# State space layer of a decoder trunk: response matrices stored lag by lag, their loads a tile ahead, prep's small products in fours

## The chip, the cores and the metric

The kernel runs on one core of a Trainium2 chip. The metric is the time of one execution on the device in microseconds (us). Three runs of the kernel before took 2993.37, 2993.86 and 2994.96 us; the median is 2993.86 us.

## The reference

The network is a trunk of two layers over 256 tokens of width 2048. Each layer has a token mixer, a cross-attention to a memory of 256 rows and a squared-ReLU MLP of width 8192. Layer 0's mixer is a gated MLP over chunks; layer 1's is a state space layer, and the change is there alone. Cut to that mixer:

```python
def s5_glu(h, w_in, lam_re, lam_im, log_dt, bm_re, bm_im, cm_re, cm_im, d_skip, w_out, b_out):
    u = (h @ w_in).reshape(bsz, seq, 128, 16)              # 128 groups of 16 channels
    lam = lax.complex(jnp.minimum(lam_re, -1e-4), lam_im)  # 128 x 64 states
    lam_bar = jnp.exp(lam * jnp.exp(log_dt)[:, None])
    b_bar = ((lam_bar - 1.0) / lam)[..., None] * bmat
    bu = jnp.einsum('gpc,bsgc->sbgp', b_bar, u)
    states[s] = lam_bar * states[s - 1] + bu[s]            # a scan over the tokens
    y = jnp.einsum('gcp,sbgp->bsgc', cmat, states).real + d_skip * u
    val, gate = jnp.split(gelu(y) @ w_out + b_out, 2, axis=-1)
    return val * jax.nn.sigmoid(gate)
```

## The kernel before

**The weight stream.** Every large product streams its weights in tiles of 256 rows by 512 columns (512 KB). For each tile, SP loads `wraw` (four buffers), ACT writes the rounded high part `whi` (L97), DVE the remainder `wlo` (L98; three buffers each), and PE multiplies in three passes. A tile costs 24 matmuls of 256 columns in `gemm_feat` (L159) and 12 matmuls of 512 columns in `gemm_tok` (L140 to L142) and `gemm_hid` (L552 to L554). After each tile, `tick` traces what is due beside the stream: pieces that `at(delay, fn)` planned for that count of tiles, and one queued piece of `self.side`, with a priority lowered by `lag`.

**What sets the order.** A scheduler places the instructions of each engine by these priorities and its own estimate of readiness. The order within an engine is then fixed; waits on semaphores are added where one engine needs another.

**Preparation.** `ssm_prep` queues the state space's matrices beside layer 0's MLP. A scan over chunks of T = 8 tokens needs three kinds of matrices, made for 32 quads (one group of 16 channels from each of four channel tiles) and kept in DRAM, two quads to a DRAM tile: `Pd` (inputs of a chunk to its state), `Qd` (state to outputs) and `Kd` (the response inside a chunk, 15 lags of 16 x 16, seven of them zero). In `quad_q`, DVE makes `qt` in three steps (L781 to L783), PE multiplies it with `bb` in four small products (L792), one into each strip of 32 rows of a PSUM tile; ACT and DVE copy them to `kd` (L796, L797), and POOL stores `kd` (L799): 128 rows of 240 numbers, a run of 960 bytes each. Only 16 rows of each 32 are read later. The same POOL queue zeroes the next `kd` (L795), loads the inputs `bcq` (L762) and stores `Qd` and `Pd` (L789, L810).

**The layer.** In `s5`, four chunks of 512 columns of `b_w_in` are streamed, eight weight tiles each, and the chain of chunk n runs beside the stream of the next one: `inputs`, `own` (products with `pq`, L874), `states`, `carry`, `outputs` (products with `dq`, L925, and with `qq`, L931), `features`. `own` and `outputs` load the matrices themselves where they are traced, through POOL (L832): `pq` from `Pd` (four buffers), `dq` from `Kd` (three) and `qq` from `Qd` (two), 512 KB each. `dq` is a Toeplitz matrix read out of `Kd` by an overlapping access pattern; each of its 128 rows is put together from eight runs of 512 bytes.

Of the kernel before, what the change touches and what calls it, by code (L numbers as in the profile page):

```python
# [9 lines left out]
F32 = mybir.dt.float32  # L10
# [6 lines left out]
P = 128  # L17
# [3 lines left out]
NB = 512  # L21
NCH = D // NB
KB = 2
# [6 lines left out]
T = 8  # L30
# [6 lines left out]
class Trunk:  # L37
    """Products run as three float32r passes over operands split exactly into a
    12-bit high part and the remainder; the residual stream stays on chip,
    token-major, and weights are streamed in chunks of KB x 128 rows by 512  # L40
    columns."""
# [26 lines left out]
    def later(self, n):  # L68
        """What is traced inside gives way to what the stream traces next."""
        return self.tc.high_priority(offset=-n)  # L70

    def at(self, delay, fn):
        """Trace fn after that many more pieces of the weight stream."""
        self.plan.append((self.now + delay, len(self.plan), fn))
        self.plan.sort(key=lambda p: p[:2])

    def tick(self):
        """Trace what is due beside the weight stream: planned pieces, then one queued piece."""
        self.now += 1
# [44 lines left out]
    def gemm_tok(self, act, w, n, acc=None, k0=0, kts=range(KT), first=True, last=True, raw=None):  # L124
        """acc[tok, t, col] (+)= act^T @ w[:, chunk n]"""
        nc = self.nc
        ah, al = act
        if acc is None:
            acc = self.psA.tile([P, 2, NB], F32, name="acc")
        out = acc if isinstance(acc, list) else [acc[:, t, :] for t in range(2)]  # L130
        kts = list(kts)
        for i in range(0, len(kts), KB):
            hi, lo = self.wtile(w, n, (k0 + kts[i]) // KB, raw)
            for kk in range(KB):
                kt = kts[i + kk]
                st = first and i == 0 and kk == 0
                en = last and i + kk == len(kts) - 1
                for t in range(2):
                    sl = slice(t * P, (t + 1) * P)
                    nc.tensor.matmul(out[t], ah[:, kt, sl], hi[:, kk, :], start=st, stop=False)  # L140
                    nc.tensor.matmul(out[t], ah[:, kt, sl], lo[:, kk, :], start=False, stop=False)  # L141
                    nc.tensor.matmul(out[t], al[:, kt, sl], hi[:, kk, :], start=False, stop=en)  # L142
            self.tick()
        return acc

    def gemm_feat(self, act, w, n):
        """acc[f, ft, tok] = (w[:, chunk n])^T @ act"""
        nc = self.nc
        ah, al = act
        acc = self.psA.tile([P, 4, S], F32, name="acc")  # L150
        for kc in range(KT // KB):
            hi, lo = self.wtile(w, n, kc)
            for kk in range(KB):
                kt = kc * KB + kk
# [46 lines left out]
    def transpose_chunk(self, src, gi, act, j, permute=False, halves=(0, 1)):  # L201
        """act[:, 4j..4j+3, :] = (src[tok, t, 512])^T * g, split"""
# [20 lines left out]
    def scale_chunk(self, src, gi, act, j):  # L223
        """act[:, 4j..4j+3, :] = src[feature, kt, token] * g, split"""
# [17 lines left out]
    def mem_stats(self, pool):  # L242
        """1/rms of each memory row, per partition and along the free axis"""
# [14 lines left out]
    def mem_prep(self, pool, layer):  # L258
        """Queue memory * g, feature-major, beside the stream; 1/rms comes later."""
# [320 lines left out]
    def exp(self, pool, x, shape, name, tag=None):  # L580
        """exp(x): n ln2 taken off in two exact parts, a polynomial, 2^n from the bits."""
# [22 lines left out]
    def cos_sin(self, pool, th, shape):  # L604
        """cos and sin: a multiple of pi/2 taken off in three parts, polynomials,
        then the quadrant's turn."""
# [37 lines left out]
    def ssm_prep(self, pool):  # L644
        """Queue the making of the chunked form of the state space, per group of 16 channels:
        Pd: lam^jr B_bar, rows (jr, c), from inputs of a chunk to its state;
        Qd: C lam^(j+1), columns (j, c), from the state before a chunk to its outputs;
        Kd: C lam^lag B_bar (+ d at lag 0), the response inside a chunk, after T-1 zero lags.
        A quad is one group of each 128-channel tile; two quads share a DRAM tile."""
# [7 lines left out]
        self.Kd = mk("Kd", [32, 2, 4, NL, 16])  # L657
# [81 lines left out]
        def last():  # L739
            """lam^8, lam^16, lam^32: over one, two and four chunks"""  # L740
# [14 lines left out]
        def cols(q):  # L755
            """the four groups of quad q: one in each 128-channel tile"""
            g0 = 32 * (q // 8) + q % 8
            return slice(g0, g0 + 25, 8)
# [26 lines left out]
        def quad_q(q):  # L785
# [5 lines left out]
            for g in range(4):  # L791
                nc.tensor.matmul(kp[32 * g:32 * g + 32], bb[:, g], qt[:, 0:T, g, :], start=True, stop=True,  # L792
                                 skip_group_check=True)
# [5 lines left out]
            nc.gpsimd.dma_start(out=self.Kd[q // 2][:, q % 2].rearrange("k t l c -> t k (l c)"), in_=kd)  # L799
# [22 lines left out]
    def s5(self, x, cur, nxt):  # L822
# [3 lines left out]
        with tc.tile_pool(name="s5", bufs=2, reuse_waits="tile") as sp:  # L826
# [3 lines left out]
            def load(src, nm):  # L830
                t = sp.tile([P, 2, 4, P], F32, name=nm, bufs={"pq": 4, "dq": 3, "qq": 2}[nm])
                nc.gpsimd.dma_start(out=t, in_=src)  # L832
                return t

            def chunks(n, acc):
                """Tokens to chunks: rows of u are (channel tile, chunk)."""
# [26 lines left out]
            def own(n):  # L863
                """each chunk's own part of its state"""
# [3 lines left out]
                for h in range(2):  # L868
                    pz = self.ps([P, 2, 2, 2, 64])
                    for i in range(2):  # L870
                        pq = load(self.Pd[4 * n + 2 * h + i], "pq")
# [8 lines left out]
            def states(n):  # L880
                """rows of vv are (odd group, state), real and imaginary apart"""
# [14 lines left out]
            def carry(n, c, k, by=1):  # L896
                """vv[c] += lam^(8 by) vv[c - by] for c, c + 2 by, ..., k of them"""
# [13 lines left out]
            def outputs(n, half):  # L911
# [4 lines left out]
                row = (2 * T - 1) * 16  # L916
                for i in (2 * half, 2 * half + 1):
                    kd = self.Kd[4 * n + i]
                    dq = load(bass.AP(tensor=kd.tensor, offset=kd.offset,
                                      ap=[[16, T], [8 * row, 16], [row, 8], [1, P]]), "dq")  # L920
                    qq = load(self.Qd[4 * n + i].rearrange("l p r n -> (l p) r n"), "qq")
                    qv = qq.rearrange("p r a b -> p r (a b)").rearrange("p r (j t c) -> p r t j c", t=4, c=16)
                    for l in range(2):
                        for t in range(4):
                            nc.tensor.matmul(py[l][32 * t:32 * t + 32, i, :], us[:, 2 * i + l, t, :], dq[:, l, t, :],  # L925
# [8 lines left out]
            def features(n):  # L934
                py = st.pop(n)[2]
                y = sp.tile([P, T, 4, 2, 16], F32, name="y", bufs=1)
# [11 lines left out]
            def follow(n):  # L948
                """the chain of channel tiles 4n..4n+3, laid beside the stream"""
# [10 lines left out]

            for n in range(NCH):
# [8 lines left out]
            for j in range(NCH):  # L970
# [20 lines left out]
                val = sp.tile([P, 2, NB], F32, name="val", bufs=1)  # L991
                gat = sp.tile([P, 2, NB], F32, name="gat", bufs=1)
# [14 lines left out]
class Norm:  # L1007
    """The RMSNorm of x that the next part reads: x is transposed and scaled by
    g chunk by chunk as it is finished; 1/rms comes later, per token."""
# [17 lines left out]
class FinalNorm:  # L1027
    """x * g and the sums of squares as the chunks of x are finished; then, per token tile,
    1/rms and the output."""
# [33 lines left out]
def regroup(tr, x):  # L1063
    """x in the order the state space wants: row (q, c) of tile h is token 8c + 4h + q."""
# [43 lines left out]
def chunked(w):  # L1108
    """[..., K, N] -> [..., N / 512, K / (KB 128), 128, KB, 512]"""
# [51 lines left out]
```

## Time and profile before

| | |
|---|---|
| median of three runs | 2993.86 us |
| span of the profiled execution, first to last instruction | 2994.1 us |
| time of PE, DVE, ACT, POOL busy | 2924.3, 1769.5, 1312.2, 168.9 us |
| mean granted TensorE clock | 0.991 of full speed |
| preparation: first to last small product L792 | 812.1 to 1412.0 us |
| state space layer: first to last load of `dq` or `qq` | 1490.0 to 1707.5 us |

PE is TensorE's matmul queue, PEld its weight loads, DVE VectorE, ACT ScalarE, POOL GpSimd and SP SyncE. A line such as L792 is a line of the kernel before. In a row of a group, the first number behind the bar is busy time, the second the mean of one instruction in ns, and behind the next bar stands the idle time just before these instructions with what ended it. A busy PE is not PE at its peak: its matmuls are pipelined, and what counts is how far apart they start.

### The profile page before, as it was taken

The numbers are of one execution on the slowest core, as the hardware profiler recorded it, in microseconds if no ns is written. First come the engines' busy times: TensorE is split into PE (matmuls) and PEld (weight loads), VectorE is DVE, ScalarE is ACT, GpSimd is POOL, SyncE is SP. The second block draws the span as 40 slices with busy tenths as digits, with TensorE's granted clock in tenths as the row PEclk, the third lists the DMA queues.
The fourth block names the chain that finished last, engine by engine and source line by source line (L and its number), as shares of the span: only waits on it lengthen the run. The fifth ranks groups of instructions, "written<-read, shape, count | busy, mean of one in ns | idle before, by whom it ended". The sixth has DMA issues, their size and how long they took to land.

```text
span 2994.1 us, 45200 instructions
## 1 busy us (share of the span) xinstructions
PE 2924.3 (98%) x18310; PEld 2552.0 (85%) x18310; DVE 1769.5 (59%) x2372; ACT 1312.2 (44%) x1602; POOL 168.9 (6%) x288
## 2 busy tenths in 40 slices
PE   8999999999999999999997899999999999999998
PEld 6788999889879879789875688999889889898996
DVE  6665645585677677676565455645555555554455
ACT  6444544445434434334453344544444434343343
POOL 1000000000011111110002100000000000000000
PEclk9999999999999999999998999999999999999999
DMA  8665555557666666666689956655565565565564
GB/s 289 209 192 183 187 173 176 169 183 231 187 203 205 198 202 207 200 201 193 210 237 234 213 175 210 190 170 177 169 189 183 184 188 184 186 183 187 185 184 152
DMA packets 180482, 581.98 MB, mean 194 GB/s; under 512 B 38592, under 2 KB 38896, under 8 KB 179504
## 3 DMA queue, kind: packets, MB, share of 16 engines
q1 hardware_dynamic: 140864, 509.67, 54.3%
q0 software_dynamic: 39264, 69.35, 9.0%
q8 instruction: 143, 2.34, 0.3%
q14 instruction: 67, 0.55, 0.1%
q10 hardware_dynamic: 144, 0.07, 0.0%
HBM read 553.88 MB, written 24.90 MB: 193 GB/s over the span
## 4 chain that ended last, share of the span: by engine, by line
PE 89%; DMA 5%; issue 3%; DVE 2%; ACT 1%; POOL 0%; SPq 0%; DVEq 0%; ACTq 0%; POOLq 0%
PE acc L159 37%; PE acc L553 8%; PE acc L554 8%; PE acc L552 8%; PE acc L141 7%; PE acc L142 7%; PE acc L140 7%; PE ps L792 1%; DMA dq<-Kd 1%; DMA qq<-Qd 1%; PE ps L488 1%; PE ps L432 1%; DVE wlo L98 1%; PE ps L210 1%; DMA memc<-in_mem 1%
## 5 line engine op out<-in xcount | busy, mean ns | idle before, releaser
L98 DVE TENSOR_TENSOR wlo<-wraw,whi 128x1024 fp32r<-128x1024 f32 x952 | 1164.1, 1223 | 987.3 <-ACT whi L97 985.3
L97 ACT CAST whi<-wraw 128x1024 fp32r<-128x1024 f32 x952 | 998.5, 1050 | 1366.7 <-PE acc L159 536.6
L159 PE MATMUL acc<-act_h,wlo 128*128 128x256 f32 x3072 | 875.1, 285 | 1.4 <-DVE wlo L98 1.4
L159 PE MATMUL acc<-act_l,whi 128*128 128x256 f32 x3072 | 875.0, 285 | 0.0
L159 PE MATMUL acc<-act_h,whi 128*128 128x256 f32 x3072 | 873.9, 284 | 0.2 <-ACT whi L97 0.2
L159 PEld LDWEIGHTS acc<-act_h,wlo 128*128 128x128 f32 x3072 | 588.9, 192 | 8.3 <-issue 6.5
L159 PEld LDWEIGHTS acc<-act_l,whi 128*128 128x128 f32 x3072 | 589.3, 192 | 4.8 <-issue 4.4
L159 PEld LDWEIGHTS acc<-act_h,whi 128*128 128x128 f32 x3072 | 589.0, 192 | 4.6 <-issue 3.8
L141 PE MATMUL acc<-wlo,act_h 128*128 128x512 f32 x1248 | 492.4, 395 | 11.8 <-DVE wlo L98 11.5
L140 PE MATMUL acc<-whi,act_h 128*128 128x512 f32 x1248 | 493.8, 396 | 9.6 <-ACT whi L97 9.6
L142 PE MATMUL acc<-whi,act_l 128*128 128x512 f32 x1248 | 490.2, 393 | 0.0
L553 PE MATMUL acc<-wlo,hh 128*128 128x512 f32 x992 | 397.2, 400 | 0.0
L552 PE MATMUL acc<-whi,hh 128*128 128x512 f32 x992 | 394.6, 398 | 0.0
L554 PE MATMUL acc<-whi,hl 128*128 128x512 f32 x992 | 393.9, 397 | 0.0
L141 PEld LDWEIGHTS acc<-wlo,act_h 128*128 128x128 f32 x1248 | 237.0, 190 | 65.2 <-DVE wlo L98 17.6
L140 PEld LDWEIGHTS acc<-whi,act_h 128*128 128x128 f32 x1248 | 236.8, 190 | 61.0 <-ACT whi L97 11.3
L142 PEld LDWEIGHTS acc<-whi,act_l 128*128 128x128 f32 x1248 | 236.8, 190 | 49.3 <-issue 0.6
L552 PEld LDWEIGHTS acc<-whi,hh 128*128 128x128 f32 x992 | 186.3, 188 | 48.4 <-issue 3.0
L554 PEld LDWEIGHTS acc<-whi,hl 128*128 128x128 f32 x992 | 186.3, 188 | 48.0 <-issue 4.2
L553 PEld LDWEIGHTS acc<-wlo,hh 128*128 128x128 f32 x992 | 186.3, 188 | 46.4 <-issue 3.2
L792 PE MATMUL ps<-qt,bb 128*32 128x128 f32 x256 | 51.2, 285 | 0.0
L536 DVE SCALAR_TENSOR_TENSOR x<-acc,r,x 128x512 f32<-128x512 f32 x62 | 43.6, 746 | 10.1 <-PE acc L554 10.1
(287 smaller groups left out, 1672.5 us busy)
## 6 DMA issues: line engine op xcount, KB each, us to landing
wraw<-in_f_w_up SPq DMA_DIRECT2D x256, 512.0 KB, 3.6
wraw<-in_f_w_down SPq DMA_DIRECT2D x256, 512.0 KB, 3.6
wraw<-in_x_w_kv SPq DMA_DIRECT2D x128, 512.0 KB, 3.5
wraw<-in_a_w_in SPq DMA_DIRECT2D x64, 512.0 KB, 4.4
wraw<-in_x_w_q SPq DMA_DIRECT2D x64, 512.0 KB, 3.6
wraw<-in_x_w_o SPq DMA_DIRECT2D x64, 512.0 KB, 3.5
wraw<-in_b_w_out SPq DMA_DIRECT2D x64, 512.0 KB, 4.4
wraw<-in_a_w_out SPq DMA_DIRECT2D x32, 512.0 KB, 3.5
```

The lines of the kernel that those rows point to most:

```text
L97: self.nc.scalar.copy(out=hi, in_=src)
L98: self.nc.vector.tensor_tensor(out=lo, in0=src, in1=hi.bitcast(F32), op=ALU.subtract)
L140: nc.tensor.matmul(out[t], ah[:, kt, sl], hi[:, kk, :], start=st, stop=False)
L141: nc.tensor.matmul(out[t], ah[:, kt, sl], lo[:, kk, :], start=False, stop=False)
L142: nc.tensor.matmul(out[t], al[:, kt, sl], hi[:, kk, :], start=False, stop=en)
L159: mm = lambda s, m, b, e: nc.tensor.matmul(acc[:, f, :], s, m, start=b, stop=e, skip_group_check=True)
L210: nc.tensor.transpose(pt[:, kk, t * P:(t + 1) * P], src[:, t, c:c + P], self.ident)
L536: nc.vector.scalar_tensor_tensor(out=xc, in0=acc[:, t, :], scalar=r2[:, t:t + 1], in1=xc, op0=ALU.mult, op1=ALU.add)
L552: nc.tensor.matmul(acc[:, t, :], ah[:, kt % 4, sl], hi[:, kk, :], start=st, stop=False)
L553: nc.tensor.matmul(acc[:, t, :], ah[:, kt % 4, sl], lo[:, kk, :], start=False, stop=False)
L554: nc.tensor.matmul(acc[:, t, :], al[:, kt % 4, sl], hi[:, kk, :], start=False, stop=en)
L792: nc.tensor.matmul(kp[32 * g:32 * g + 32], bb[:, g], qt[:, 0:T, g, :], start=True, stop=True, skip_group_check=True)
```

## The change

1. **Fours.** The four small products of a quad stand in a block of higher priority (`high_priority(offset=2 * self.lag)`), so that the scheduler gives them precedence over the stream instead of after it.
2. **`Kd` lag by lag.** The DRAM tile is now [16, 15 lags, 2, 4, 16]: for each input channel and lag, the 128 numbers of two quads lie side by side. Only the 16 rows that are read are stored, in four DMAs, one for each channel tile, of 240 runs of 64 bytes each: 960 runs and 60 KB for a quad in place of 128 runs and 120 KB.
3. **Loads of `dq`.** A row of `dq` is now one run of 4 KB, since eight lags lie behind each other: 128 runs for a load in place of 1024.
4. **Loads ahead.** `fetch` loads `pq`, `dq` and `qq` by the plan (`at`) some eight weight tiles before their use, from the chunk ahead; `dq` and `qq` have four buffers each. `y` shares `z`'s buffer, `val` and `gat` those of `pq`.
5. Comments and docstrings are gone, so that lines shift by up to 21; the small products are L794, the store of `kd` is L802, the loads L837, the products with `dq` and `qq` L939 and L945.

```diff
@@ ssm_prep
-        self.Kd = mk("Kd", [32, 2, 4, NL, 16])
+        self.Kd = mk("Kd", [16, NL, 2, 4, 16])
@@ quad_q
-            for g in range(4):
-                nc.tensor.matmul(kp[32 * g:32 * g + 32], bb[:, g], qt[:, 0:T, g, :], start=True, stop=True,
-                                 skip_group_check=True)
+            with self.tc.high_priority(offset=2 * self.lag):
+                for g in range(4):
+                    nc.tensor.matmul(kp[32 * g:32 * g + 32], bb[:, g], qt[:, 0:T, g, :], start=True, stop=True,
+                                     skip_group_check=True)
...
-            nc.gpsimd.dma_start(out=self.Kd[q // 2][:, q % 2].rearrange("k t l c -> t k (l c)"), in_=kd)
+            for t in range(4):
+                nc.gpsimd.dma_start(out=self.Kd[q // 2][:, :, q % 2, t], in_=kd[32 * t:32 * t + 16])
@@ s5
+            ahead = {}
+
-            def load(src, nm):
-                t = sp.tile([P, 2, 4, P], F32, name=nm, bufs={"pq": 4, "dq": 3, "qq": 2}[nm])
+            def load(src, nm, shape):
+                t = sp.tile(shape, F32, name=nm, bufs={"pq": 4, "dq": 4, "qq": 4}[nm])
                 nc.gpsimd.dma_start(out=t, in_=src)
                 return t
 
+            def fetch(nm, n, i):
+                if nm == "pq":
+                    t = load(self.Pd[4 * n + i], nm, [P, 2, 4, P])
+                elif nm == "qq":
+                    t = load(self.Qd[4 * n + i].rearrange("l p r n -> (l p) r n"), nm, [P, 2, 4 * P])
+                else:
+                    kd = self.Kd[4 * n + i]
+                    t = load(bass.AP(tensor=kd.tensor, offset=kd.offset,
+                                     ap=[[P, T], [(2 * T - 1) * P, 16], [1, T * P]]), nm, [P, T * P])
+                ahead[nm, n, i] = t
@@ own
-                        pq = load(self.Pd[4 * n + 2 * h + i], "pq")
+                        pq = ahead.pop(("pq", n, 2 * h + i))
@@ outputs
-                    dq = load(bass.AP(tensor=kd.tensor, offset=kd.offset,
-                                      ap=[[16, T], [8 * row, 16], [row, 8], [1, P]]), "dq")
-                    qq = load(self.Qd[4 * n + i].rearrange("l p r n -> (l p) r n"), "qq")
+                    dq = ahead.pop(("dq", n, i)).rearrange("p (j l t c) -> p l t j c", j=T, l=2, t=4)
+                    qq = ahead.pop(("qq", n, i))
...
-                            nc.tensor.matmul(py[l][32 * t:32 * t + 32, i, :], us[:, 2 * i + l, t, :], dq[:, l, t, :],
+                            nc.tensor.matmul(py[l][32 * t:32 * t + 32, i, :], us[:, 2 * i + l, t, :], dq[:, l, t],
@@ features
-                y = sp.tile([P, T, 4, 2, 16], F32, name="y", bufs=1)
+                y = sp.tile([P, T, 4, 2, 16], F32, name="y", tag="z", bufs=1)
@@ follow
+                for i in range(4):
+                    if n + 1 < NCH:
+                        self.at(4, lambda i=i: fetch("pq", n + 1, i))
+                    self.at(6 + i // 2 * 2, lambda i=i: fetch("dq", n, i))
+                    self.at(6 + i // 2 * 2, lambda i=i: fetch("qq", n, i))
...
+            for i in range(4):
+                fetch("pq", 0, i)
...
-                val = sp.tile([P, 2, NB], F32, name="val", bufs=1)
-                gat = sp.tile([P, 2, NB], F32, name="gat", bufs=1)
+                val = sp.tile([P, 2, NB], F32, name="val", tag="pq", bufs=4)
+                gat = sp.tile([P, 2, NB], F32, name="gat", tag="pq", bufs=4)
```

What the scheduler makes of this is seen in the order of the instructions on PE and on POOL.

On PE, before, the small products of the last quad lie between matmuls of the stream (L159), one and one:

```order
L159 MATMUL acc<-act_l,whi 128x256
L792 MATMUL ps<-qt,bb 32x128 [waits PE_49]
L159 MATMUL acc<-act_h,wlo 128x256
L792 MATMUL ps<-qt,bb 32x128
L159 MATMUL acc<-act_h,whi 128x256
L792 MATMUL ps<-qt,bb 32x128
L159 MATMUL acc<-act_l,whi 128x256
L792 MATMUL ps<-qt,bb 32x128
L159 MATMUL acc<-act_h,wlo 128x256
```

On PE, of the change, the same quad's products (L794) follow each other, from the start of their weight tile, which is the row that waits for ACT:

```order
L159 MATMUL acc<-act_h,whi 128x256 [waits Activation_49]
L159 MATMUL acc<-act_l,whi 128x256
L159 MATMUL acc<-act_h,wlo 128x256 [waits DVE_49]
L159 MATMUL acc<-act_h,whi 128x256
L159 MATMUL acc<-act_l,whi 128x256
L159 MATMUL acc<-act_h,wlo 128x256
L159 MATMUL acc<-act_h,whi 128x256
L794 MATMUL ps<-qt,bb 32x128 [waits DVE_49,PE_49]
L794 MATMUL ps<-qt,bb 32x128 x3
L159 MATMUL acc<-act_l,whi 128x256
```

They moved forward by eight weight tiles and stand right where the scheduler takes `qt` to be ready, behind the seventh matmul of a tile, with a wait for DVE. In all 32 quads the four stand together; on DVE the place of `qt` between the `wlo` of the stream is the same in both kernels.

On POOL, before, one round of the preparation for a quad holds one store of `kd`:

```order
L789 DMA Qd_5990<-qt 2x64x512
L799 DMA Kd_6005<-kd 4x32x240
L795 MEMSET kd 128x112
L810 DMA Pd_5973<-po 128x512
L762 DMA bcq<-in_b_bc 128x256
```

On POOL, of the change, it holds four (here a later round; the rounds are alike):

```order
L790 DMA Qd_5998<-qt 2x64x512
L802 DMA Kd_6014<-kd 240x1x16 x4
L797 MEMSET kd 128x112
L813 DMA Pd_5982<-po 128x512
L763 DMA bcq<-in_b_bc 128x256
```

The zeroing of the next `kd`, which waits for the landing of the stores ahead of it, the store of `Pd` and the load of `bcq` stand behind them as before.

On POOL, before, in the state space layer, the loads of chunk 0's third and fourth `qq` (Qd_5988, Qd_5989) and fourth `dq` come behind the `pq` of chunk 2, and chunk 1's begin between them:

```order
L832 DMA pq<-Pd_5981 128x1024
L832 DMA dq<-Kd_6005 128x8x128
L832 DMA qq<-Qd_5988 128x1024
L832 DMA qq<-Qd_5989 128x1024
L832 DMA dq<-Kd_6006 128x8x128
L832 DMA dq<-Kd_6007 128x8x128
L832 DMA qq<-Qd_5990 128x1024
```

On POOL, of the change, at the same place behind the `pq` of chunk 2, only chunk 1's eight loads stand there:

```order
L837 DMA pq<-Pd_5981 128x1024
L837 DMA dq<-Kd_6006 128x1x1024
L837 DMA qq<-Qd_5990 128x1024
L837 DMA dq<-Kd_6007 128x1x1024
L837 DMA qq<-Qd_5991 128x1024
L837 DMA dq<-Kd_6008 128x1x1024
L837 DMA qq<-Qd_5992 128x1024
L837 DMA dq<-Kd_6009 128x1x1024
L837 DMA qq<-Qd_5993 128x1024
```

Chunk 0's loads have gone ahead of it, and each load of chunk 1 waits only for the products of chunk 0 that free its buffer. The order of PE in this layer is the same in both kernels.

More of the change, by code (lines that the diff above doesn't have):

```diff
@@ L915, in outputs @@
                 py = st[n][2]
-                row = (2 * T - 1) * 16
                 for i in (2 * half, 2 * half + 1):
-                    kd = self.Kd[4 * n + i]
-                    dq = load(bass.AP(tensor=kd.tensor, offset=kd.offset,
-                                      ap=[[16, T], [8 * row, 16], [row, 8], [1, P]]), "dq")
-                    qq = load(self.Qd[4 * n + i].rearrange("l p r n -> (l p) r n"), "qq")
-                    qv = qq.rearrange("p r a b -> p r (a b)").rearrange("p r (j t c) -> p r t j c", t=4, c=16)
+                    dq = ahead.pop(("dq", n, i)).rearrange("p (j l t c) -> p l t j c", j=T, l=2, t=4)
+                    qq = ahead.pop(("qq", n, i))
+                    qv = qq.rearrange("p r (j t c) -> p r t j c", t=4, c=16)
                     for l in range(2):
                         for t in range(4):
-                            nc.tensor.matmul(py[l][32 * t:32 * t + 32, i, :], us[:, 2 * i + l, t, :], dq[:, l, t, :],
+                            nc.tensor.matmul(py[l][32 * t:32 * t + 32, i, :], us[:, 2 * i + l, t, :], dq[:, l, t],
                                              start=(i == 0), stop=False, skip_group_check=True)
```

## The prediction

> **What bounds the kernel now.** I read the page first, then stretches of the span, PE's waits and the timeline at the places that the change touches.
>
> ```profile
> span 2994.1 us, 45200 instructions
> PE 2924.3 (98%) x18310; PEld 2552.0 (85%) x18310; DVE 1769.5 (59%) x2372; ACT 1312.2 (44%) x1602; POOL 168.9 (6%) x288
> ...
> L792 PE MATMUL ps<-qt,bb 128*32 128x128 f32 x256 | 51.2, 285 | 0.0
> ```
>
> PE is busy for 98% of the span, so there are two ways to win: less time on PE, or less of its 70 us of idle time. In 900 to 1200 us (preparation beside the MLP) PE has no idle time at all; in 1500 to 1800 us, where the state space layer lies, 36 us are missing and the clock is down:
>
> ```profile
> 900.00:1200.00 300.00, 300.00 (x2000) 260.04 (x1999) 218.49 (x338) 121.67 (x138) 47.41 (x81) 1.00 0.67 203
> 1500.00:1800.00 300.00, 263.72 (x2047) 208.74 (x2046) 172.46 (x315) 136.51 (x223) 39.21 (x52) 0.93 0.82 215
> ```
>
> (The columns are length, busy time of PE, PEld, DVE, ACT and POOL, granted clock, DMA share and GB/s.) The longest in the list of PE's waits says for what (us in total, times, longest):
>
> ```profile
> PE ps L931 <- DMA qq<-Qd: 30.8, 8, 8.2
> ```
>
> 30.8 us go to the state space layer's products with `qq`, in eight waits of up to 8.2 us; every other wait of PE is for less. So the layer is bound by the loads that the change moves, and the preparation by PE itself.
>
> **The fours.** A busy PE can still be slow. The timeline of the last quad, a stream matmul of 256 columns (L159) and a small product in turn (a product has two records):
>
> ```profile
> 1389.77 0.28 PE L159 MATMUL acc<-act_h,whi 128*128 128x256 f32 x1
> 1389.89 0.28 PE L159 MATMUL acc<-act_l,whi 128*128 128x256 f32 x1
> 1390.10 0.41 PE L792 MATMUL ps<-qt,bb 128*32 128x128 f32 x2
> 1390.43 0.39 PE L159 MATMUL acc<-act_h,wlo 128*128 128x256 f32 x1
> ...
> 1392.39 0.39 PE L159 MATMUL acc<-act_h,wlo 128*128 128x256 f32 x1
> 1392.61 0.28 PE L159 MATMUL acc<-act_h,whi 128*128 128x256 f32 x1
> ```
>
> Stream matmuls alone start 0.12 us apart. From 1389.89 to 1392.61 lie five such steps, 0.60 us, yet 2.72 us pass: the four products cost 2.12 us, 0.53 us each. The array seems to run empty at each change from 128 columns to a strip of 32 and back: after 1389.89 the product starts 0.21 us later, not 0.12. What a row of such products costs, the layer's products with `pq` show, which have the same shape (128x32 by 128 columns) and stand together, 32 at once:
>
> ```profile
> 1543.87 0.47 PE L141 MATMUL acc<-wlo,act_h 128*128 128x512 f32 x1
> 1544.35 1.95 PE L874 MATMUL ps<-pq,us 128*32 128x128 f32 x64
> 1546.23 0.50 PE L142 MATMUL acc<-whi,act_l 128*128 128x512 f32 x1
> 1546.57 0.39 PE L140 MATMUL acc<-whi,act_h 128*128 128x512 f32 x1
> 1546.80 0.40 PE L141 MATMUL acc<-wlo,act_h 128*128 128x512 f32 x1
> ```
>
> From 1543.87 to 1546.80 lie three steps of 0.23 us, 0.69 us, but 2.93 us pass: 32 products cost 2.24 us. With 0.53 us for one and 2.24 for 32, each further one costs (2.24 - 0.53) / 31 = 0.055 us, and four 0.53 + 3 x 0.055 = 0.70 us. A four thus saves 1.42 us, and 32 of them **45 us**. The bounds: a four costs no less than one alone (0.53 us, 51 us saved), and no more than now (nothing saved); I take 0.70, since it rests on products of the same shape on the same strips. The Trainium skill, "TensorE: Matmul & The Clock Gate", section "Measured speedup vs the span model", gives products on different column strips one product's time and some 4 ns for each further one; by it a four would cost about 0.54 us, and the sum be 5 us lower. The run of 32 cannot decide that, since eight products share each strip there.
>
> **What the fours wait for.** Before, `qt` was done tiles ahead; now the four stand where it is only just ready, with a wait for DVE, and the whole stream on PE is queued behind them. Since DVE's order there is unchanged, the trace of before tells how late `qt` is: the end of its last step against the start of the stream matmul behind which nothing but the four would now stand. For the last quad, that is the eighth matmul of its tile; for the 19th, the one where this gap is largest:
>
> ```profile
> 1383.68 0.76 DVE L783 TENSOR_TENSOR qt<-qt,tq 128x576 f32<-128x576 f32 x1
> ...
> 1134.68 0.75 DVE L783 TENSOR_TENSOR qt<-qt,tq 128x576 f32<-128x576 f32 x1
> ```
>
> ```profile
> 1384.13 0.28 PE L159 MATMUL acc<-act_l,whi 128*128 128x256 f32 x1
> ...
> 1132.36 0.28 PE L159 MATMUL acc<-act_h,whi 128*128 128x256 f32 x1
> ```
>
> The last would wait 1384.44 - 1384.13 = 0.31 us, the 19th 1135.43 - 1132.36 = 3.07 us. Over all 32 the positive gaps sum to 7.9 us; nine quads have none. PE will also come sooner, by 1.42 us a quad, where quads follow closely and DVE has no rest. I take **10 us**; nothing is the lower bound, 1 us each (32) the upper.
>
> **The stores of `kd`.** POOL issues four instead of one, 4 x 0.72 for 0.72 us, and 960 runs of 64 bytes replace 128 of 960. Rows of POOL and DVE in 900 to 1300 us, and landings:
>
> ```profile
> L789 POOL DMA_DIRECT2D Qd<-qt x20 | 16.8, 838 | 14.3 <-DVE qt L783 12.1 <-issue 2.2
> L799 POOL DMA_DIRECT2D Kd<-kd x21 | 15.2, 723 | 147.6 <-DVE bb L771 82.7 <-DVE kd L797 35.4 <-DVE qt L781 25.1
> L810 POOL DMA_DIRECT2D Pd<-po x21 | 12.7, 604 | 19.4 <-ACT po L809 14.7 <-issue 4.0 <-ACT whi L97 0.6
> L762 POOL DMA_DIRECT2D bcq<-in_b_bc x20 | 11.3, 565 | 53.5 <-DVE tq L782 53.2 <-issue 0.3
> L795 POOL MEMSET kd<- 128x112 f32 x21 | 4.0, 191 | 108.9 <-DMA Kd<-kd 108.9
> ```
>
> ```profile
> L763 DVE TENSOR_SCALAR bcq<-bcq,sg 128x128 f32<-128x128 f32 x20 | 5.7, 285 | 26.6 <-DMA bcq<-in_b_bc 26.6
> ```
>
> ```profile
> dq<-Kd POOLq DMA_DIRECT2D x16, 512.0 KB, 17.9
> qq<-Qd POOLq DMA_DIRECT2D x16, 512.0 KB, 14.5
> ...
> Kd<-kd POOLq DMA_DIRECT2D x32, 120.0 KB, 5.5
> ...
> eye<-in_eye POOLq DMA_DIRECT2D x1, 8.0 KB, 1.8
> ```
>
> POOL stands in the zeroing of `kd` until the stores land; the load of `bcq` is behind it, and DVE already waits for `bcq` 26.6 us in 20 quads. No row shows stores of 64 bytes. The nearest by length is `eye`, 128 runs of 64 bytes in 1.8 us; the nearest by count `dq`, 1024 runs in 17.9 us, much of that in a crowd. In bytes the stores halve, so they might even land sooner. I take about 8 us, nearer to `eye`. POOL waits for DVE 53.2 us before these loads of `bcq`, 2.7 us a quad, which covers the 2.2 us of issue and part of the later landing; the rest falls on quads that follow closely. I take **3 us** on PE, from 0 to 20.
>
> **The layer's loads.** Why `qq` came late: POOL issued it at 1581.82 only because its buffer had just come free, and 512-byte runs held the queues.
>
> ```profile
> 1580.49 1.34 POOL L832 DMA_DIRECT2D dq<-Kd  x1 [4.15 <-PE ps L925]
> 1581.82 1.09 POOL L832 DMA_DIRECT2D qq<-Qd  x2
> ```
>
> ```profile
> 1580.00:1600.00 20.00, 11.93 (x209) 8.48 (x202) 14.54 (x43) 5.43 (x8) 5.77 (x7) 0.82 1.01 231
> 1600.00:1626.00 26.00, 25.31 (x257) 20.13 (x256) 12.51 (x17) 17.10 (x36) 5.69 (x8) 0.94 0.97 268
> 1626.00:1647.00 21.00, 11.86 (x126) 8.59 (x126) 12.91 (x42) 3.19 (x4) 5.21 (x8) 0.76 1.02 181
> ...
> 1673.00:1689.00 16.00, 10.70 (x123) 7.66 (x122) 10.64 (x38) 3.19 (x4) 5.54 (x6) 0.79 0.96 179
> ...
> 1707.00:1724.00 17.00, 8.69 (x110) 6.31 (x109) 4.38 (x4) 3.15 (x3) 1.05 (x2) 0.75 0.92 261
> 1724.00:1740.00 16.00, 16.00 (x94) 12.90 (x79) 4.87 (x5) 6.27 (x8) 0.00 (x0) 0.84 0.24 71
> ```
>
> The DMA share is near 1.0 while only 179 to 268 GB/s move. Of the change's loads, each is issued eight tiles before its use. Will the bytes fit? Chunks 1 and 2 need, in eight tiles, 8 x 512 KB of weights and 12 loads of 512 KB, 10.5 MB; in one chunk's round, 1580 to 1626 us, PE is busy for 11.93 + 25.31 = 37.2 us, of which 3.6 are the low clock's (next paragraph): 34 us, 309 GB/s. Where only `pq` and weights moved, in runs of 4 KB, the trace shows more:
>
> ```profile
> 1423.00:1431.00 8.00, 8.00 (x36) 6.46 (x35) 3.68 (x3) 3.09 (x3) 2.58 (x7) 1.00 0.96 337
> ```
>
> 337 is above 309, by little; but a load has some 30 us to land, and 12 of them need 6.3 MB / (337 - 124 GB/s for the weights) = 30 us. So the eight waits should go: **31 us**, of which I leave 2 for weights that come late.
>
> With them goes the low clock: around each wait the granted clock is down. Busy time times missing clock, row by row: 2.1 + 1.5 + 2.8 + 2.2 + 2.2 + 2.6 = **13 us** (none of it if the clock stays low). POOL's in-order queue holds each load behind those ahead; the last that can block it, chunk 2's `pq`, wait for products that come before those that free `dq`. What is late next is the stream: ACT and DVE, with waits of 1 us here and there.
>
> **The sum.** 2994.1 - 45 + 10 + 3 - 31 + 2 - 13 = 2920 us, against the profiled execution's own span; the median of the runs, 2993.86, is 0.2 us from it, so I predict **2920 us**. Buffers shared by `y`, `val` and `gat` cost nothing: their products stand far apart in PE's unchanged order.
>
> **The rivals.**
> - *The fours' saving goes into a new wait.* `qt` is late by 1 us on average and not 0.3, because DVE, at 218 of 300 us busy, must now keep up with a faster PE. For it: 23 of the 32 quads have no slack. Against it: 27% of DVE is free. 2920 + 22 = 2942 us.
> - *The layer stays bound by transfers.* The bytes read are the same and the share was 1.0; if contention holds the rate at 268 GB/s, half of the waits and of the low clock remain: 2920 + 22 = 2942 us. Against it: the 337 GB/s above.
> - *The change doesn't do what it says:* a four runs no faster than the products apart. 2920 + 45 - 10 = 2955 us. Against it: the 32 products in 2.24 us.
> - *Slower: the stores of 64 bytes pace the preparation.* A round of POOL is 0.84 + 4 x 0.72 + landing + 0.19 + 0.60 + 0.57 = 5.1 us and the landing; a quad of the faster stream has some 17.8 us ((1383.7 - 1134.7) / 13 by the `qt` rows, less 1.4). From a landing of 12.7 us on, DVE waits for `bcq` in every round, and PE for DVE. With `dq`'s 17.9 us, 32 x 5.2 = 166 us: 3086 us. The Trainium skill speaks for it: "DMA: Bandwidth & Descriptors", section "Specifications", says that a transfer of under 512 bytes is done as a read-modify-write; no run here shows what that costs. Against it: `eye`.
>
> **How the numbers follow.** Chances: forecast 0.66, new wait 0.14, transfers 0.09, no gain from fours 0.04, stores 0.07. The forecast's own range is 2900 to 2935. The range to report reaches down to 2898 (51 us from the fours, 5 us of waits) and up to 2952, over both 2942 cases; outside are the stores, the upper tails of the two rivals and a little below: under 0.2. A measurement of this kernel can tell about 0.2%, 6 us, from no change. All cases but the stores are faster by more: 0.93. Of the stores' 0.07, a landing just above 12.7 us gives back all and no more: same 0.02, slower 0.05.
>
> **What would show it.** L794 in groups of four with the next stream matmul some 0.7 us on, beyond the wait; PE's waits on DVE `qt` of about 10 us in all; no waits on `qq`; clock at 1.00 through the layer; `dq` landing in about 6 us as `pq` does; `kd` stores landing in under 12 us. Wrong would make it: PE idle in 900 to 1400 us of far more than 15 us, or waits of L939 and L945 on DMA.

## The result, and the profile after

The change made the kernel slower: 3110.54 us, median of four runs (3103.84 to 3113.96), against 2994.41 us before (2993.37 to 2996.88, four runs). The ratio is 1.038, with a 95% interval of 1.0368 to 1.0400. The forecast was 2920 us, faster. The page of the changed kernel, to be read against the rows shown above:

```profile
span 3112.2 us, 45452 instructions
...
PE 2933.0 (94%) x18310; PEld 2581.5 (83%) x18310; DVE 1762.7 (57%) x2372; ACT 1315.1 (42%) x1602; POOL 205.8 (7%) x384
...
PE   8999999999877887888899999999999999999998
...
PEclk9999999999988898888999999999999999999999
...
L782 DVE TENSOR_TENSOR qt<-T,bcq 128x576 f32<-128x576 f32 x32 | 24.3, 758 | 229.4 <-DMA Qd<-qt 229.4
```

Before, PE was busy for 98% of the span. Now slices 11 to 20 of 40 (some 780 to 1560 us), which are the preparation beside the MLP, show 7 and 8, and in slices 15 to 22 the clock is mostly 8. One group is new among the costliest although it is busy for only 24.3 us: the first step of `qt` on DVE (L782), with 229.4 us of idle time ahead of it, all of it ended by the landing of a store, `Qd<-qt`.

How much each part of the program gained or lost is read from two stretches that hold the same work in both kernels: from about the 257th to the 485th split of a weight tile (`wlo`), which is nearly all of the preparation, and from there to about the 537th, which is the state space layer. Windows of the kernel before, and then of the changed one (columns as in the prediction):

```profile
785.00:1515.00 730.00, 730.00 (x4321) 611.02 (x4320) 508.42 (x763) 303.08 (x356) 99.78 (x168) 1.00 0.66 203
...
1515.00:1748.00 233.00, 196.76 (x1741) 153.55 (x1740) 127.13 (x256) 100.43 (x173) 32.31 (x42) 0.90 0.86 215
```

```profile
782.00:1662.00 880.00, 745.54 (x4317) 643.79 (x4316) 500.47 (x761) 303.61 (x356) 146.75 (x265) 0.91 0.54 164
...
1662.00:1866.00 204.00, 189.57 (x1744) 148.81 (x1743) 127.69 (x258) 100.72 (x173) 22.16 (x41) 0.97 0.89 251
```

The layer gained 233 - 204 = 29 us. The preparation lost 880 - 730 = 150 us: PE, which never stood there before, is idle for 880 - 745.5 = 134.5 us, and the clock is 0.91. What PE waits for in the first of these stretches:

```profile
PE acc L159 <- DVE wlo L98: 55.6, 17, 5.1
PE acc L553 <- DVE wlo L98: 51.5, 12, 5.5
PE ps L794 <- DVE qt L784: 27.1, 12, 4.1
```

Only 27.1 us are the wait that the prediction priced, that of the fours for `qt`. The other 107 us are waits of the weight stream for DVE's splits, and the timeline of DVE shows why DVE is late. The row in brackets is the idle time ahead and what ended it:

```profile
1023.84 0.75 DVE L784 TENSOR_TENSOR qt<-qt,tq 128x576 f32<-128x576 f32 x1
...
1025.64 0.23 DVE L799 SCALAR_TENSOR_TENSOR kd<-eye,dsk,ps 128x16 f32<-128x16 f32 x1
...
1026.78 0.29 DVE L764 TENSOR_SCALAR bcq<-bcq,sg 128x128 f32<-128x128 f32 x1 [0.31 <-DMA bcq<-in_b_bc]
1035.60 0.76 DVE L782 TENSOR_TENSOR qt<-T,bcq 128x576 f32<-128x576 f32 x1 [8.53 <-DMA Qd<-qt]
1036.27 3.49 DVE L98 TENSOR_TENSOR wlo<-wraw,whi 128x1024 fp32r<-128x1024 f32 x3
```

```profile
1024.90 0.83 POOL L790 DMA_DIRECT2D Qd<-qt  x1 [1.34 <-DVE qt L784]
1026.46 2.28 POOL L802 DMA_DIRECT2D Kd<-kd  x4 [0.72 <-issue]
```

```profile
1037.55 0.58 PE L159 MATMUL acc<-act_h,wlo 128*128 128x256 f32 x1 [4.73 <-DVE wlo L98]
```

DVE finishes one quad's `qt` at 1024.59, and POOL (second fence) issues its store at 1024.90. At 1027.07 DVE comes to the first step of the `qt` two quads on. There are two buffers of `qt`, so this step writes the buffer that is being stored, and it may not begin before the store has landed. DVE stands for 8.53 us, and since it takes its instructions in order, three splits of weight tiles queue behind it; they run back to back from 1036.27, and PE (third fence) had nothing to do for 4.73 us. So DVE stands in 30 of 32 quads.

That step has moved. This is DVE's order from the 11th quad's last step of `qt`, the one of this timeline, to the first step of the 13th, which takes the same buffer (`qt<-T_6023,bcq`, the last row); first before, with all splits of the stream between the two kept, then of the change:

```
L783 TENSOR_TENSOR qt<-qt,tq 128x4x9x16
L98 TENSOR_TENSOR wlo<-wraw,whi 128x1024
L782 TENSOR_TENSOR tq<-T_6024,bb 128x4x128
L763 TENSOR_SCALAR bcq<-bcq,sg 128x128
L98 TENSOR_TENSOR wlo<-wraw,whi 128x1024
...
L98 TENSOR_TENSOR wlo<-wraw,whi 128x1024 x2
...
L98 TENSOR_TENSOR wlo<-wraw,whi 128x1024
L782 TENSOR_TENSOR tq<-T_6024,bcq 128x576
L783 TENSOR_TENSOR qt<-qt,tq 128x4x9x16
L782 TENSOR_TENSOR tq<-T_6024,bb 128x4x128
L98 TENSOR_TENSOR wlo<-wraw,whi 128x1024
L763 TENSOR_SCALAR bcq<-bcq,sg 128x128
L98 TENSOR_TENSOR wlo<-wraw,whi 128x1024
...
L98 TENSOR_TENSOR wlo<-wraw,whi 128x1024
...
L98 TENSOR_TENSOR wlo<-wraw,whi 128x1024
L771 TENSOR_TENSOR bb<-F,bcq 128x4x16 x2
L797 SCALAR_TENSOR_TENSOR kd<-eye,dsk,ps 128x16
L781 TENSOR_TENSOR qt<-T_6023,bcq 128x4x9x16
```

```
L784 TENSOR_TENSOR qt<-qt,tq 128x4x9x16
L98 TENSOR_TENSOR wlo<-wraw,whi 128x1024
L799 SCALAR_TENSOR_TENSOR kd<-eye,dsk,ps 128x16
L783 TENSOR_TENSOR tq<-T_6024,bb 128x4x128
L764 TENSOR_SCALAR bcq<-bcq,sg 128x128
L782 TENSOR_TENSOR qt<-T_6023,bcq 128x4x9x16
```

In both, the step stands behind `kd` of the quad two back (the last `kd` row), because the small products that make that `kd` are, beside the store, the last readers of the buffer. Before, these products were spread over the stream, and from the `qt` whose buffer it takes to the step lay 4 to 15 splits of the stream, here 9. The list of DMAs of the kernel before has the store (KB each, median us from issue to landing):

```profile
Qd<-qt POOLq DMA_DIRECT2D x32, 256.0 KB, 11.6
```

The step came at the earliest 15 us after the store was issued, so the store had landed each time. The fours let go of the buffer at once, and the step moved up to one split, seldom two, once four, behind the `qt` that is being stored.

### The profile page after: what moved, and what is told of

Its sections match the earlier page's. It is cut to its first block, busy times and chain, and to the rows that moved or that the text cites. A ratio compares the mean times of both kernels' runs of the same rounds, so it can differ in the third digit from the quotient of the medians.

```text
span 3112.2 us, 45452 instructions
## 1 busy us (share of the span) xinstructions
PE 2933.0 (94%) x18310; PEld 2581.5 (83%) x18310; DVE 1762.7 (57%) x2372; ACT 1315.1 (42%) x1602; POOL 205.8 (7%) x384
## 4 chain that ended last, share of the span: by engine, by line
PE 73%; DMA 13%; DVE 6%; issue 5%; ACT 2%; POOL 1%; SPq 0%; DVEq 0%; POOLq 0%; ACTq 0%
PE acc L159 29%; DMA Qd<-qt 8%; PE acc L141 7%; PE acc L142 7%; PE acc L140 7%; PE acc L553 6%; PE acc L554 6%; PE acc L552 5%; DVE wlo L98 3%; DMA Kd<-kd 2%; ACT whi L97 1%; DMA wraw<-in_b_w_in 1%; PE ps L488 1%; PE ps L432 1%; PE ps L210 1%
## 5 line engine op out<-in xcount | busy, mean ns | idle before, releaser
L159 PE MATMUL acc<-act_h,wlo 128*128 128x256 f32 x3072 | 888.2, 289 | 56.0 <-DVE wlo L98 56.0
L159 PE MATMUL acc<-act_l,whi 128*128 128x256 f32 x3072 | 885.6, 288 | 0.0
L159 PE MATMUL acc<-act_h,whi 128*128 128x256 f32 x3072 | 884.4, 288 | 0.0
L159 PEld LDWEIGHTS acc<-act_h,wlo 128*128 128x128 f32 x3072 | 602.2, 196 | 62.6 <-DVE wlo L98 59.6
L159 PEld LDWEIGHTS acc<-act_l,whi 128*128 128x128 f32 x3072 | 601.9, 196 | 1.8 <-issue 1.4
L159 PEld LDWEIGHTS acc<-act_h,whi 128*128 128x128 f32 x3072 | 602.3, 196 | 0.8 <-issue 0.4
L140 PE MATMUL acc<-whi,act_h 128*128 128x512 f32 x1248 | 491.9, 394 | 11.6 <-ACT whi L97 10.0
L553 PE MATMUL acc<-wlo,hh 128*128 128x512 f32 x992 | 408.2, 411 | 51.5 <-DVE wlo L98 51.5
L552 PE MATMUL acc<-whi,hh 128*128 128x512 f32 x992 | 402.6, 406 | 0.0
L782 DVE TENSOR_TENSOR qt<-T,bcq 128x576 f32<-128x576 f32 x32 | 24.3, 758 | 229.4 <-DMA Qd<-qt 229.4
L802 POOL DMA_DIRECT2D Kd<-kd x128 | 72.6, 582 | 44.0 <-issue 41.4
```

Of the source, the lines that this page charges most:

```text
L159: mm = lambda s, m, b, e: nc.tensor.matmul(acc[:, f, :], s, m, start=b, stop=e, skip_group_check=True)
L552: nc.tensor.matmul(acc[:, t, :], ah[:, kt % 4, sl], hi[:, kk, :], start=st, stop=False)
L553: nc.tensor.matmul(acc[:, t, :], ah[:, kt % 4, sl], lo[:, kk, :], start=False, stop=False)
L802: nc.gpsimd.dma_start(out=self.Kd[q // 2][:, :, q % 2, t], in_=kd[32 * t:32 * t + 16])
```

## The experiments

Two theories were put against each other. **A**: the landing of the store of `Qd` holds the buffer of `qt`, and DVE waits for it in order. **B**, the rival from the prediction: the stores of `kd` in 64-byte runs pace POOL, and with it the preparation. (C and D, on the layer, come with the fifth experiment.)

**One more buffer.** The changed kernel with

```diff
-            qt = pool.tile([P, T + 1, 4, 16], F32, name="qt", bufs=2)
+            qt = pool.tile([P, T + 1, 4, 16], F32, name="qt", bufs=3)
```

> The changed kernel with a third buffer of qt. Theory A (DVE stands in the first step of qt, L782, until the store of Qd from the same buffer has landed, about 8 us in 30 quads; the scheduler puts that step as early as a buffer seems free): in DVE's order the step moves up one quad more, and again stands just behind the store whose buffer it takes, so nothing is gained: 3110 us (3085 to 3130), DVE's wait for Qd in L782 still about 200 us. Theory A' (one buffer too few, plainly): the wait goes, about 2930 us. Theory B (the 64-byte stores of kd pace POOL and with it the preparation): 3110 us, with POOL's wait for Kd as before.

Measured: 3104.84 us (3103.38 to 3106.25), 1.037 of before (1.0349 to 1.0390). DVE's waits:

```profile
DVE qt L782 <- DMA Qd<-qt: 215.0, 28, 9.4
```

A buffer more changes next to nothing: the scheduler moves the step one quad further ahead, again one or two tiles behind the store whose buffer it takes. This is what A says, and B cannot be told from it here; A', that one buffer is simply missing, is out.

**Two more buffers.** The same line with `bufs=4`.

> The changed kernel with four buffers of qt. In DVE's order L782 stands where it does with three, but waits for the store of one quad earlier, some 18 us old. Theory A: DVE's wait for Qd in L782 falls from 229 us to under 20, PE's waits for wlo in 750 to 1500 us go, the clock there is 1.00 again; about 2925 us (2910 to 2950). Theory B: the stores of kd are unchanged, so the time stays above 3050 us.

Measured: 2930.44 us (2926.61 to 2940.74), 0.9793 of before (0.9768 to 0.9818). The window of the same work, PE's waits in it of over 0.5 us, and DVE's group of the step:

```profile
784.00:1482.00 698.00, 683.77 (x4312) 596.56 (x4312) 502.71 (x762) 302.04 (x356) 147.48 (x267) 1.00 0.71 209
```

```profile
PE ps L794 <- DVE qt L784: 12.4, 14, 2.5
PE acc L159 <- DVE wlo L98: 0.9, 2, 0.5
```

```profile
L782 DVE TENSOR_TENSOR qt<-T,bcq 128x576 f32<-128x576 f32 x32 | 24.2, 756 | 0.8
```

The step stands in DVE's order where it did with three buffers, give or take a tile, mostly right behind the scaling of its `bcq`; but with four buffers the store that it waits for is a quad older. When DVE comes to the step, that store was issued 20.7 us earlier in the median and 14.2 us at the least, and none took longer than 13.2 us to land. The 229 us are gone, the clock is 1.00, and the stores of `kd` are untouched. This decides for A against B. It also splits the loss. The same work takes 880 us in the changed kernel and 698 us here, 182 us less. Of these, 745.5 - 683.8 = 62 us are PE's busy time, the low clock that came with the waits (by the granted clock, an estimate of 0.09 x 745.5 = 67 us), and 134.5 - 14.2 = 120 us are idle time, the waits themselves. Against 730 us before, the busy time is 46 us less: that is what the fours save.

**Without the fours.** The changed kernel with its small products at their old priority.

```diff
-            with self.tc.high_priority(offset=2 * self.lag):
-                for g in range(4):
+            for g in range(4):
```

> The changed kernel without the fours: the small products at their old priority, everything else of the change kept (stores of kd in four, loads ahead). In DVE's order the first step of qt stands again 4 to 15 tiles behind the store whose buffer it takes. Theory A: no wait for Qd in L782, the preparation takes what it took before, plus 3 us for the stores; the layer keeps its gain of 30 to 42 us: about 2960 us (2945 to 2972). Theory B: the 64-byte stores still pace POOL's round: above 3050 us.

Measured: 2966.32 us (2962.03 to 2968.23), 0.9905 of before (0.9887 to 0.9923). The window of the preparation, and how the stores land there (KB each, median us from issue to landing):

```profile
785.00:1514.00 729.00, 729.00 (x4313) 610.14 (x4312) 508.27 (x763) 302.59 (x356) 146.62 (x265) 1.00 0.67 199
```

```profile
Qd<-qt POOLq DMA_DIRECT2D x32, 256.0 KB, 11.6
...
Kd<-kd POOLq DMA_DIRECT2D x128, 15.0 KB, 4.6
```

The preparation takes what it took before, to 1 us, with four times as many stores of `kd`. With the kernel of four buffers, which has these stores too, theory B is out; of the 3 us that the prediction gave the stores nothing shows.

**The fours alone.** The kernel before with only that priority added, its one store of `kd` and its loads kept.

```diff
-            for g in range(4):
+            with self.tc.high_priority(offset=2 * self.lag):
+                for g in range(4):
```

> The kernel before with the fours alone (priority of the small products): one store of kd, in its old layout, and the old loads. Theory A: the wait for Qd in L782 comes with the fours, about 8 us in 30 quads; the preparation loses about 150 us and the layer gains nothing: about 3145 us (3110 to 3165). Theory B: no 64-byte stores, so nothing paces POOL: 2994 - 45 + 10 = about 2960 us.

Measured: 3144.61 us (3136.92 to 3151.20), 1.0502 of before (1.0477 to 1.0527). DVE's and PE's waits:

```profile
DVE qt L781 <- DMA Qd<-qt: 231.2, 30, 10.4
```

```profile
PE ps L932 <- DMA qq<-Qd: 28.3, 8, 7.3
```

The whole loss comes with the fours, in a kernel without any of the new stores, and the layer's old waits are there beside it.

**The layer: layout or time of issue.** Two halves of the change, each taken out of the kernel with four buffers of `qt`. Theory **C**: the loads being issued eight tiles ahead is what gains. Theory **D**, the prediction's: the 512-byte runs held the queues. First the old layout, with one store of `kd` (of the diff, the tile and the load):

```diff
-        self.Kd = mk("Kd", [16, NL, 2, 4, 16])
+        self.Kd = mk("Kd", [32, 2, 4, NL, 16])
...
-                                     ap=[[P, T], [(2 * T - 1) * P, 16], [1, T * P]]), nm, [P, T * P])
+                                     ap=[[16, T], [8 * row, 16], [row, 8], [1, P]]), nm, [P, 2, 4, P])
```

> Against e2 (four buffers of qt, 2930 us): Kd in its old layout, one store of kd with 960-byte runs, loads of dq with 512-byte runs; all loads still issued a tile ahead. Theory C (what gained in the layer is only that loads are issued eight tiles ahead; the layout bought nothing, since dq still lands in about 16 us with 4-KB runs): 2930 us (2918 to 2942), no PE wait on dq or qq of over 5 us in all. Theory D (the prediction's: 512-byte runs hold the queues, so that without the layout about half of the waits for qq and of the low clock stay): 2947 to 2965 us. If the 64-byte stores of kd cost the preparation anything, this one also shows it, as a gain.

Then the new layout, with each load where it is used (of the diff, the new calls; the loads by the plan no longer happen, and `dq` and `qq` have the three and two buffers of before, so that issue and buffers change together):

```diff
-                        pq = ahead.pop(("pq", n, 2 * h + i))
+                        fetch("pq", n, 2 * h + i)
+                        pq = ahead.pop(("pq", n, 2 * h + i))
...
+                    fetch("dq", n, i)
+                    fetch("qq", n, i)
```

> Against e2 (2930 us): Kd in its new layout, but pq, dq and qq loaded where they are used, with the buffers of before (4, 3, 2). Theory C (the time of issue counts): the layer is as before, 8 waits of PE for qq, 30 us in all, and the clock down: 2930 + 33 = 2963 us (2952 to 2972). Theory D (the runs' length counts): half or more of the gain stays, 2930 to 2947 us.

Measured: 2940.91 us (2940.31 to 2943.93) with the old layout, 0.9822 of before (0.9807 to 0.9837), and 2958.37 us (2956.60 to 2959.32) with late loads, 0.9877 (0.9860 to 0.9894). The windows of the layer with four buffers alone, with the old layout, with late loads, and, for scale, of the fours alone, whose layer is that of before:

```profile
1482.00:1679.00 197.00, 186.25 (x1745) 146.99 (x1744) 127.82 (x257) 100.64 (x174) 21.03 (x39) 0.99 0.90 254
```

```profile
1486.00:1694.00 208.00, 192.03 (x1745) 150.71 (x1744) 128.18 (x257) 101.09 (x174) 29.88 (x39) 0.96 0.93 241
```

```profile
1482.00:1711.00 229.00, 197.93 (x1741) 154.22 (x1741) 127.19 (x256) 100.28 (x173) 22.71 (x42) 0.91 0.83 223
```

```profile
1660.00:1889.00 229.00, 196.72 (x1745) 153.58 (x1744) 127.96 (x259) 100.50 (x174) 32.28 (x42) 0.90 0.87 220
```

The layer of before takes 229 to 233 us. With late loads the new layout gains nothing to speak of (229), early loads with the old one gain 21 to 25 us (208), both together 32 to 36 (197). So C holds in the main: early issue, with the buffers that it needs, gains most. What the layout is worth once the loads are early is less sure. `dq` lands in 21.7 us with the old one and 16.4 us with the new, and the two windows differ by 11 us; but five other profiles of the layer with the new layout and early loads take 199 to 205 us for the same stretch, so that 3 us is as well supported as 11, and the runs of the two kernels touch (2940.31 at the least, 2940.74 at the most). The preparation takes 702 us with one store of `kd` a quad, against 698 us with four: nothing is gained by going back to one.

**The landing itself.** In the changed kernel the store of `Qd` takes more than twice as long as that of `Pd`, which has as many bytes:

```profile
Qd<-qt POOLq DMA_DIRECT2D x32, 256.0 KB, 10.7
Pd<-po POOLq DMA_DIRECT2D x32, 256.0 KB, 4.6
```

The store of `Qd` stands in the order of POOL as 2x64x512, that of `Pd` as 128x512. The changed kernel, with its two buffers of `qt`, and

```diff
-            nc.gpsimd.dma_start(out=self.Qd[q // 2][q % 2].rearrange("p r n -> r p n"), in_=qt[:, 1:])
+            for r in range(2):
+                nc.gpsimd.dma_start(out=self.Qd[q // 2][q % 2][:, r], in_=qt[64 * r:64 * r + 64, 1:])
```

> The changed kernel, two buffers of qt, with the store of Qd issued as two of 64 partitions each instead of one with the two halves as its outer dimension. In the trace of the changed kernel the last packets of that store go out at 12 per us of 159 ns each, which is about two DMA engines' work, while the store of Pd, as many bytes, lands in 4.6 us. Theory A: if the two halves land in about 5 us instead of 10.7, DVE's wait for Qd in L782 falls from 229 us to under 60 us and the time to 2945 us (2928 to 2985), with nothing changed in DVE's order but a tile. If the landing stays at 10 us, the time stays near 3100 us. Theory B (stores of kd): stays above 3050 us in both cases.

Measured: 2925.89 us (2923.95 to 2928.81), 0.9771 of before (0.9756 to 0.9786). Landings, and DVE's wait:

```profile
Qd<-qt POOLq DMA_DIRECT2D x64, 128.0 KB, 3.6
...
Kd<-kd POOLq DMA_DIRECT2D x128, 15.0 KB, 3.8
```

```profile
DVE qt L782 <- DMA Qd<-qt: 25.9, 18, 5.0
```

Two lines turn the slower kernel into one that is 2.3% faster than before, with DVE's step still one or two splits behind the store: the halves land in 3.6 us each, and from the first issue to the second landing it is 4.6 us in the median. The `kd` stores gain with it; that in the changed kernel (8.2 us) they queued behind the tail of `Qd` fits, since they land in 4.6 us without the fours, where they stand apart from it.

**Both cures.** Four buffers of `qt` and the store in two.

> Four buffers of qt (e2) and the store of Qd in two. Theory A: no wait for Qd is left to shorten in DVE; the stores of kd land sooner, since they no longer queue behind Qd's tail (9.5 us in e2, 4.6 us in e3 where they stood apart), so POOL is back at the load of bcq sooner and DVE's 41.7 us of waits for bcq shrink, with them some of PE's 12.4 us of waits for qt: 2922 us (2912 to 2932). If nothing of this reaches PE: 2930 us.

Measured: 2921.51 us (2916.68 to 2924.39), 0.9754 of before (0.9737 to 0.9771), the fastest of all. The waits that it was to shorten:

```profile
DVE bcq L764 <- DMA bcq<-in_b_bc: 28.3, 20, 3.7
```

```profile
PE ps L795 <- DVE qt L784: 6.1, 14, 2.7
```

With four buffers alone these were 41.7 and 12.4 us. The 9 us between the medians are in line with that, though the runs of the two kernels come from two sets and lie 2 us apart at the nearest.

## Why the prediction was wrong

**The step that failed** is the one on what the fours wait for: "Since DVE's order there is unchanged, the trace of before tells how late `qt` is". Only the last step of `qt` kept its place in DVE's order; of this one alone the sentence on DVE in the section on the change holds too. The first step, which takes the buffer, moved from 4 to 15 tiles behind a store that lands in 11.6 us to one or two behind it, where DVE stands for it, 229 us in all. The number that was needed stood in the list of DMAs of before, as a landing that cost nothing there. The prediction priced what the fours wait for, but not what they set free and who would take it, and where. Its own terms for the preparation, -45 + 10 + 3 = -32 us, are what the kernel with four buffers shows (698 against 730 us); what it lacked is a term of +182 us, 120 us of waits and 62 us of low clock, and it gave 0.05 to anything slower. Its own sign for being wrong, "PE idle in 900 to 1400 us of far more than 15 us", is what the windows show.

**The fours: -45 us was right.** PE's busy time for the same work falls from 730 to 684 us, by 46 us. In the kernel with four buffers, a four in the timeline:

```profile
1071.20 0.39 PE L553 MATMUL acc<-wlo,hh 128*128 128x512 f32 x1
1071.43 0.40 PE L554 MATMUL acc<-whi,hl 128*128 128x512 f32 x1
1071.86 0.43 PE L794 MATMUL ps<-qt,bb 128*32 128x128 f32 x8
1072.22 0.50 PE L552 MATMUL acc<-whi,hh 128*128 128x512 f32 x1
1072.55 0.39 PE L553 MATMUL acc<-wlo,hh 128*128 128x512 f32 x1
1072.78 0.40 PE L554 MATMUL acc<-whi,hl 128*128 128x512 f32 x1
```

From 1071.43 to 1072.78 lie three steps of 0.23 us, 0.69 us, and 1.35 us pass: 0.66 us for the four, where 0.70 was forecast. The 0.54 us that the prediction estimated from the Trainium skill, "TensorE: Matmul & The Clock Gate", section "Measured speedup vs the span model", is too low for all that the stream loses here, of which 0.1 us is the slower step behind the four.

**Their wait for `qt`: +10 us** was right once DVE is not held up otherwise: 12.4 us with four buffers, 8.1 us with the store in two; 27.1 us in the changed kernel.

**The stores of `kd`: +3 us** was too much; they cost nothing that could be measured, and land in 3.7 to 4.6 us where they do not queue behind a long store of `Qd`, with 8 us forecast. The rival built on them gave 3086 us, nearest of all to the result, by a mechanism that the runs rule out.

**The layer: -42 us** was too large, for a mechanism that was half right. The eight waits for `qq` are gone, and the clock rose. But it is the early issue, with its buffers, that removes them: with late loads and runs of 4 KB, eight waits for `qq` were left, 24.5 us in all, so that "512-byte runs held the queues" was the lesser part. In the changed kernel the stretch gained 29 us. PE's idle time fell from 36.2 to 14.4 us, by 21.8 us, where the sum has 31 - 2 = 29. Its busy time, in which the low clock shows, fell from 196.8 to 189.6 us, by 7.2 us, where the sum has 13; busy time times missing clock, by which the 13 us were sized, falls from 19.7 to 5.7 us and so says about twice what was gained. The idle time that is left is in part a wait that grew: PE waited for `u` of ACT for 2.7 us before (L860), and for 9.2 us in the changed kernel (L877). With four buffers of `qt` the gain was 36 us, 25.5 us of it idle time and 10.5 us busy time. `dq` landing in about 6 us was wrong: it took 15.6 us with runs of 4 KB, and only its early issue hides that.

**The sum** with the sizes as measured, for four buffers of `qt`: 2994.1 - 46 + 14 (PE's idle time in the preparation) + 0 - 36 = 2926 us, against a span of 2924.9. For the changed kernel: 2994.1 + 150 - 29 - 3 (the stream reaches the preparation 3 us earlier) = 3112, its span.

## What to carry to other kernels

When a change lets an engine finish with a buffer sooner, look for the instruction that takes the buffer next, in its own engine's order, and not only for the one that waits for the result: here the scheduler put it right behind the store that still read the buffer. Where a store reads that buffer, the row of its landing says how long an in-order engine would stand, and the cure is a faster landing or enough buffers that the store waited for is a whole round old; one buffer more did next to nothing here. A landing that is much longer than another of as many bytes is worth a look even while it costs nothing.

## What was unexpected of the hardware

- One store lands in 10.6 to 11.7 us in the median or, as two halves, in 4.6 us. In the trace of the changed kernel, of the 4-KB packets of 159 ns some 11 to 13 go out per us at the end of the store that is issued at 1024.90: the work of about two of 16 DMA engines (12 x 0.159 = 1.9). The Trainium skill has the rule, "DMA: Bandwidth & Descriptors", section "Rules for kernel authors": an outermost dimension of fewer than 16 keeps the whole transfer on at most that many engines. The trace agrees for the 2 of `Qd`. By the same rule `dq`, whose 8 rows of lags are the outermost dimension in DRAM, would use at most 8 engines; that it lands in 15.6 us and `pq`, as many bytes, in 6.4 fits, but other loads stood beside it, and its dimensions were not changed in a run.
- Short waits cost the clock as well: 134.5 us of idle time, in waits of at most 5.5 us, came with a granted clock of 0.91 instead of 1.00 and 62 us more of busy time for the same work.
- Stores in runs of 64 bytes cost nothing to be seen here, though the Trainium skill, "DMA: Bandwidth & Descriptors", section "Specifications", says that they are done as read-modify-writes: 15 KB in such runs land in 3.7 to 4.6 us, when nothing slow is ahead of them; whether they are done that way no run here shows.
- Why the scheduler takes the buffer to be free so early was not looked into; that it reckons with a shorter landing than the chip's is likely, and not shown.
